# Projections in steps of three matmuls, a solve one slot later, and PSUM tiles read by one engine each, in a hybrid RWKV-7 and S5 block

## The chip, the cores and the metric

The kernel runs on one core of one Trainium2 chip. The metric is device time in microseconds (us) of one execution, and less is better. Before the change the median of three runs is 2781.7 us (2778.65 to 2786.51).

## The reference, cut to what matters

One layer on 2048 frames of width 1024: a norm, one wide input projection, an RWKV-7 branch (16 heads of 64), an S5 branch, gates, output projections and a residual. Nearly all matmul work is projections; the change lies around the chunked form of the RWKV-7 recurrence.

```python
h = rms_norm(x, norm_g[l]); z = h @ w_in[l]
zs, gate_a, u, gate_b, m_a, m_b = jnp.split(z, SPLIT_POINTS, axis=-1)
...
def frame_step(S, inp):                      # wkv7: 2048 frames in order
    r_t, w_t, k_t, v_t, a_t, b_t = inp
    sa = jnp.einsum('bhij,bhj->bhi', S, a_t)
    S = S * w_t[:, :, None, :] + sa[..., None] * b_t[:, :, None, :] + v_t[..., None] * k_t[:, :, None, :]
    return S, jnp.einsum('bhij,bhj->bhi', S, r_t)
...
merged = sigmoid(m_a) * (y_a @ p_a[l]) + sigmoid(m_b) * (y_b @ p_b[l])
x = x + merged @ w_out[l]
```

## The kernel before

The RWKV branch is cut into 32 units: a pair of heads p (8 pairs, 128 channels) by a block of 512 frames (4 blocks, two at a time). A unit is eight chunks of 64 frames. The driver loop at the end of the kernel goes over units, and for each over 24 **slots**. In a slot it emits, in this order: one step of `scan` of this unit, one step of `prep2` of the next unit, at some slots a step of `sums`, one step of `prep1` of the unit after that (from slot 13, P1) and of `post2` of the unit before, and then projection matmuls out of the generator `gm`, which `stream` makes of a list of jobs. Every engine runs its instructions in the order in which they are emitted, so what stands in a slot on TensorE (PE), VectorE (DVE) and ScalarE (ACT) is set by this loop; waits between engines come from the tiles that they share.

**scan** is the recurrence, three slots to a chunk. Slot 0, 3, 6, ...: matmul px from the state tile SU, which DVE copies to rh. Slot 1, 4, ...: matmul pu from rh; its two diagonal 64x64 blocks, scaled by dd, go into SU, the upper by DVE and the lower by ACT. Slot 2, 5, ...: matmul pn from SU; two DVE instructions make the next chunk's SU of it. So each slot's scan matmul needs what another engine made of the last slot's, and whatever PE has to do in a slot hides that.

**Projections** go out by `Job.run`: three 128x512 matmuls for each of 8 slices of the contraction (whi by hhi, whi by hlo, wlo by hhi), and a `yield` after every six. A slot takes one yield (six matmuls), the four slots in DOUBLE (1, 9, 15, 21) take two; 168 in a unit.

**prep2** prepares the next unit: transposes of BK (slot 1), two groups of 16 small matmuls into pairs of PSUM tiles A (slots 2 and 3), which are masked or scaled by dd into AT, then the DRAM round trip AT, ld, IX (slot 4), the product pv and the start of SU (slot 5), and from slot 6 a **solve**: 62 DVE instructions on TM, RF and IX that `Woven` puts between other DVE instructions, six a slot (SOLVE). At slot 16 the result RF goes to DRAM (rd) and back as R; after GAP slots, at slot 20, DVE transposes R into T, one half there and the other in slot 21; in slots 22 and 23 come small matmuls pz and pr. The tiles of the pool `psm` (tag m: A, sums, pv, pz and others) turn over three PSUM buffers.

**sums** makes column sums (slot 3), copies them to rows, the upper 32 rows by DVE and the lower by ACT (slot 4), sends them through DRAM and ends with a product on POOL.

## Time and profile before

| | us |
|---|---|
| median of three runs | 2781.7 |
| the profiled execution | 2781.73 |
| its span, first to last instruction | 2780.0 |
| PE busy | 2577.7 |
| DVE busy | 1923.0 |
| ACT busy | 1409.1 |
| POOL busy | 632.4 |

The units take from about 148 us to about 2170 us of the span; what is before is the first norm and projections, what is after is the S5 branch and the output projections. A timeline row gives start, duration, engine, line, operation, tiles and shapes, and in brackets the idle time before it and who ended it. An `xN` in it merges N instructions of one kind. A row of a view by line gives busy time, the mean of one instruction and the idle time just before.

### The profile page before, as it was taken

How to read it: one execution, taken by the hardware profiler on the slowest of the kernel's cores; microseconds unless marked ns; L12 is line 12 of the kernel's file. 1: busy time of each engine (PE TensorE's matmuls, PEld its weight loads, DVE VectorE, ACT ScalarE, POOL GpSimd, SP SyncE). 2: the span in 40 equal slices, each digit the busy share in tenths (PEclk: the TensorE clock that was granted, in tenths of full speed). 3: DMA queues.
4: the chain of work that ended last, by engine and by line, in shares of the span. 5: the costliest groups of instructions: out<-in, count | busy, mean ns of one | idle time of the engine just before them, and what ended most of it. 6: DMA issues, size and time to landing. Idle time of an engine off the chain costs nothing. (4 is left out here: it accounts for less than half of the span.)

```text
span 2780.0 us, 47342 instructions
## 1 busy us (share of the span) xinstructions
PE 2577.7 (93%) x16140; PEld 2044.4 (74%) x16140; DVE 1923.0 (69%) x5620; ACT 1409.1 (51%) x3547; POOL 632.4 (23%) x989
## 2 busy tenths in 40 slices
PE   6999999999999988999999999999989989999998
PEld 5777777777777766777777777777767777777777
DVE  5656677777667777766777766677768788755544
ACT  6455555555555665655555555555544443423321
POOL 3221222122222333222222122221332200111110
PEclk9999999999999999999999999999999999999999
DMA  3322333232232433333323232332466656755533
GB/s 110 78 77 66 92 77 99 70 85 78 75 92 69 136 116 100 89 82 83 86 75 92 72 90 74 88 91 71 110 180 183 212 139 168 227 185 173 168 108 98
DMA packets 256343, 303.42 MB, mean 109 GB/s; under 512 B 159745, under 2 KB 172134, under 8 KB 255078
## 3 DMA queue, kind: packets, MB, share of 16 engines
q1 hardware_dynamic: 210502, 150.94, 20.1%
q0 software_dynamic: 45600, 149.46, 18.1%
q8 instruction: 128, 2.10, 0.3%
q14 instruction: 113, 0.93, 0.1%
HBM read 219.91 MB, written 71.70 MB: 105 GB/s over the span
## 5 line engine op out<-in xcount | busy, mean ns | idle before, releaser
L950 ACT ACTIVATE SU<-pu,dd 64x64 f32<-64x64 f32 x256 | 79.0, 308 | 401.7 <-DVE SU L75 302.6
L879 DVE TENSOR_TENSOR TM<-RF,IX 128x60 f32<-128x60 f32 (+24 forms) x992 | 236.7, 239 | 64.7 <-DMA IX<-ld 42.4
L883 DVE TENSOR_TENSOR RF<-RF,TM 128x60 f32<-128x60 f32 (+24 forms) x992 | 217.2, 219 | 28.6 <-DVE TM L879 0.4
L945 ACT ACTIVATE AR<-SU,dec 64x64 f32<-64x64 f32 x512 | 176.2, 344 | 75.3 <-DVE SU L961 67.7
L953 PEld LDWEIGHTS pn<-SU,BT 128*128 128x128 f32 x512 | 86.4, 191 | 130.2 <-ACT SU L950 119.4
L953 PE MATMUL pn<-SU,BT 128*128 128x128 f32 x512 | 112.6, 302 | 67.9 <-ACT SU L950 66.0
L75 DVE TENSOR_TENSOR AT<-A,amask 64x256 f32<-64x256 f32 (+1 forms) x256 | 102.3, 419 | 72.2 <-ACT AT L843 66.9
L961 DVE SCALAR_TENSOR_TENSOR SU<-pn,dec,AR 64x64 f32<-64x64 f32 x240 | 65.3, 272 | 116.7 <-PE pn L953 116.5
L940 PEld LDWEIGHTS px<-SU,AT 128*128 128x128 f32 x512 | 93.5, 193 | 70.5 <-issue 31.4
L75 DVE COPY rh<-px 128x128 f32<-128x128 f32 x256 | 74.0, 289 | 98.5 <-PE px L940 94.3
L948 PEld LDWEIGHTS pu<-rh,R 128*128 128x128 f32 x512 | 92.3, 189 | 57.6 <-DVE rh L75 37.2
L940 PE MATMUL px<-SU,AT 128*128 128x128 f32 x512 | 104.1, 285 | 31.1 <-DVE SU L75 29.9
L843 ACT ACTIVATE AT<-A,dd 64x64 f32<-64x64 f32 x512 | 116.5, 303 | 19.0 <-PE A L837 16.3
L948 PE MATMUL pu<-rh,R 128*128 128x128 f32 x512 | 103.4, 284 | 18.7 <-DVE rh L75 17.7
L491 PE MATMUL ppa<-yhi,whi_pa 128*128 128x512 f32 x256 | 115.8, 452 | 1.4 <-ACT whi_pa L224 1.4
L491 PE MATMUL pv<-hhi,whi_v 128*128 128x512 f32 x256 | 111.5, 436 | 2.0 <-ACT carry L444 2.0
L491 PE MATMUL pmb<-hhi,whi_mb 128*128 128x512 f32 x256 | 112.0, 438 | 0.0
L491 PE MATMUL pga<-hhi,whi_ga 128*128 128x512 f32 x256 | 111.2, 434 | 0.0
L491 PE MATMUL pk<-hhi,whi_k 128*128 128x512 f32 x256 | 110.3, 431 | 0.7 <-ACT carry L444 0.7
L491 PE MATMUL pr<-hhi,whi_r 128*128 128x512 f32 x256 | 110.5, 432 | 0.0
L491 PE MATMUL pma<-hhi,whi_ma 128*128 128x512 f32 x256 | 110.1, 430 | 0.0
L493 PE MATMUL ppa<-yhi,wlo_pa 128*128 128x512 f32 x256 | 104.4, 408 | 1.6 <-DVE wlo_pa L75 1.6
(376 smaller groups left out, 7947.2 us busy)
## 6 DMA issues: line engine op xcount, KB each, us to landing
IX<-ld SPq DMA_DIRECT2D x128, 128.0 KB
raw_pa<-in_p_a_dram POOLq DMA_DIRECT2D x64, 256.0 KB, 4.3
raw_mb<-in_w_in_dram POOLq DMA_DIRECT2D x50, 256.0 KB, 3.5
raw_r<-in_w_in_dram POOLq DMA_DIRECT2D x36, 256.0 KB, 3.8
raw_k<-in_w_in_dram POOLq DMA_DIRECT2D x36, 256.0 KB, 3.6
raw_v<-in_w_in_dram POOLq DMA_DIRECT2D x36, 256.0 KB, 3.4
raw_ga<-in_w_in_dram POOLq DMA_DIRECT2D x34, 256.0 KB, 3.4
ce<-cw SPq DMA_DIRECT2D x16, 514.0 KB
```

Source lines behind the costliest of these rows:

```text
L75: r = f(*a, **kw)
L491: pe.matmul(ps, hi[:, k, :], xhi[:, kk_, :], start=(kk_ == 0), stop=False)
L493: pe.matmul(ps, lo[:, k, :], xhi[:, kk_, :], start=False, stop=(kk_ == 7))
L843: act.activation(out=at[HS[h], c, 0, h, :], in_=pas[h][HS[h], i, 0:C], func=AF.Copy, scale=dd[HS[h], c:c + 1])
L879: raw_dve.tensor_tensor(out=tm[:, 0:na, 0:nt], in0=rf[:, 0:na, s:s + 1].to_broadcast([P, na, nt]), in1=ix[:, s:s + 1, s + 1:32].to_broadca ...
L883: raw_dve.tensor_tensor(out=rf[:, 0:na, s + 1:32], in0=rf[:, 0:na, s + 1:32], in1=tm[:, 0:na, 0:nt], op=ALU.add)
L940: pe.matmul(px[:, 0:P], at[:, c, 0].rearrange("p h t -> p (h t)"), cur, start=True, stop=True)
L945: act.activation(out=us[HS[h]], in_=cur[HS[h], HS[h]], func=AF.Copy, scale=dec[HS[h]])
L948: pe.matmul(pu[:, 0:P], r64[:, c].rearrange("p h t -> p (h t)"), rh, start=True, stop=True)
L950: act.activation(out=cur[64:128, 64:128], in_=pu[64:128, 64:128], func=AF.Copy, scale=dd[64:128, c:c + 1])
L953: pe.matmul(pn[:, 0:P], bt[:, c].rearrange("p h j -> p (h j)"), cur, start=True, stop=True)
L961: (raw_dve if h == 0 else dve).scalar_tensor_tensor(out=nxt, in0=pn[HS[h], HS[h]], scalar=dec[HS[h]], in1=us[HS[h]], op0=ALU.mult, op1=ALU ...
```

## The change

The driver takes projections in steps of three matmuls: `Job.run` yields "half" after the first and third slice of four, the table HALVES says how many steps of three each slot takes (three where it says nothing; still 56, that is 168 matmuls, in a unit), and a wrapper `Steps` skips the halves for callers that want six. The loading of IX is emitted one slot earlier, the solve begins one slot later (slot 7, so it ends in slot 17), and GAP falls from 4 to 3, so T stays at slot 20. Three pairs of PSUM readers become one: the blocks of pu go by ACT alone, the rows of sums by ACT alone, and the dd blocks of A by DVE, four chunks in one instruction where ACT used one for each. Two products go from POOL to DVE (rdec, rkb), and the third and fourth step of sums come a slot later.

```diff
-GAP = 4
+GAP = 3
-DOUBLE = (1, 9, 15, 21)
+HALVES = {1: 2, 2: 1, 3: 0, 4: 2, 13: 2, 17: 1, 22: 0, 23: 0}
...
@@ Job.run
                                     next(self.bg, None)
                                 yield
+                            elif k < 3:
+                                yield "half"
...
@@ stream
-                for y, _ in enumerate(j.run()):
+                y = -1
+                for part in j.run():
+                    if part:
+                        yield part
+                        continue
+                    y += 1
...
@@ sums
+            lo_, hi_ = 0 if b else 32, 64 if a else 32
+            act.copy(rows[lo_:hi_], ps[lo_:hi_])
             if b:
-                dve.tensor_copy(rows[0:32], ps[0:32])
                 sp.dma_start(out=sd[0:2, :], in_=rows[0:2, :])
             if a:
-                act.copy(rows[32:64], ps[32:64])
...
-                pool.tensor_tensor(out=rkv_, in0=rkb, in1=U[a]["v"], op=ALU.mult)
+                dve.tensor_tensor(out=rkv_, in0=rkb, in1=U[a]["v"], op=ALU.mult)
...
@@ prep2
-                    for i in range(4):
-                        c = 4 * c2 + i
-                        act.activation(out=at[HS[h], c, 0, h, :], in_=pas[h][HS[h], i, 0:C], func=AF.Copy, scale=dd[HS[h], c:c + 1])
+                    dve.tensor_tensor(out=at[HS[h], cs_, 0, h, :], in0=pas[h][HS[h], :, 0:C], in1=dd[HS[h], cs_].unsqueeze(2).to_broadcast([C, 4, C]), op=ALU.mult)
...
-                yield
-            ix = u1.tile([P, 32, 32], F32, tag="BK", name="IX" + n)
...
-            pool.tensor_tensor(out=ar[:, :, C:2 * C], in0=ar[:, :, C:2 * C], in1=u["rdec"].to_broadcast([P, NC, C]), op=ALU.mult)
-            yield
+                    ix = u1.tile([P, 32, 32], F32, tag="BK", name="IX" + n)
...
+                yield
+            dve.tensor_tensor(out=ar[:, :, C:2 * C], in0=ar[:, :, C:2 * C], in1=u["rdec"].to_broadcast([P, NC, C]), op=ALU.mult)
...
+            yield
+            yield
             dve.chain = solve()
...
@@ scan
-                dve.tensor_scalar(out=cur[0:64, 0:64], in0=pu[0:64, 0:64], scalar1=dd[0:64, c:c + 1], scalar2=None, op0=ALU.mult)
-                act.activation(out=cur[64:128, 64:128], in_=pu[64:128, 64:128], func=AF.Copy, scale=dd[64:128, c:c + 1])
+                for h in range(2):
+                    act.activation(out=cur[HS[h], HS[h]], in_=pu[HS[h], HS[h]], func=AF.Copy, scale=dd[HS[h], c:c + 1])
...
@@ the driver
-                    if slot in (3, 4, 6 if last else 7, 11):
+                    if slot in (3, 4, 6 if last else 8, 12):
...
-                        if next(gm, None):
+                        if gm.half() == 1:
                             break
                         credit -= 1
```

On PE, slot 7 of the thirteenth unit before the change: pu, six projection matmuls (L491 to L493, of the job that fills pmb), and slot 8's pn.

```order
L948 MATMUL pu_0_2_9934<-rh_0_2_9916,R_161 128x128
L491 MATMUL pmb_0_9950<-hhi_178,whi_mb_0_9871 128x512
L492 MATMUL pmb_0_9950<-hlo_179,whi_mb_0_9871 128x512
L493 MATMUL pmb_0_9950<-hhi_178,wlo_mb_0_9872 128x512
L491 MATMUL pmb_0_9950<-hhi_178,whi_mb_0_9871 128x512
L492 MATMUL pmb_0_9950<-hlo_179,whi_mb_0_9871 128x512
L493 MATMUL pmb_0_9950<-hhi_178,wlo_mb_0_9872 128x512
L953 MATMUL pn_0_2_9957<-SU_0_9194,BT_0_9053 128x128
```

The same slot of the same unit in the changed kernel, on PE:

```order
L969 MATMUL pu_0_2_9726<-rh_0_2_9710,R_161 128x128
L491 MATMUL pmb_0_9704<-hhi_178,whi_mb_1_9676 128x512
L492 MATMUL pmb_0_9704<-hlo_179,whi_mb_1_9676 128x512
L493 MATMUL pmb_0_9704<-hhi_178,wlo_mb_1_9677 128x512
L491 MATMUL pmb_0_9704<-hhi_178,whi_mb_1_9676 128x512
L492 MATMUL pmb_0_9704<-hlo_179,whi_mb_1_9676 128x512
L493 MATMUL pmb_0_9704<-hhi_178,wlo_mb_1_9677 128x512
L491 MATMUL pmb_0_9704<-hhi_178,whi_mb_1_9676 128x512
L492 MATMUL pmb_0_9704<-hlo_179,whi_mb_1_9676 128x512
L493 MATMUL pmb_0_9704<-hhi_178,wlo_mb_1_9677 128x512
L974 MATMUL pn_0_2_9753<-SU_0_8982,BT_0_8896 128x128
```

Between pu and pn stand nine projection matmuls now. The same holds for the other slots that HALVES does not name.

On DVE, slots 2 and 3 of that unit before the change: the two halves of the next SU, the four masked blocks of the first pair of tiles A, a weight's low part (wlo), and rh.

```order
L961 SCALAR_TENSOR_TENSOR SU_0_9194<-pn_0_0_9763,dec_0_8883,AR_0_8887 64x64
L75 SCALAR_TENSOR_TENSOR SU_0_9194<-pn_0_0_9763,dec_0_8883,AR_0_8887 64x64
L75 TENSOR_TENSOR AT_1_9720<-A_1_0_0_9767,amask 64x4x64
L75 TENSOR_TENSOR AT_1_9720<-A_1_0_0_9767,amask 128x4x64
L75 TENSOR_TENSOR AT_1_9720<-A_1_0_1_9768,amask 64x4x64
L75 TENSOR_TENSOR AT_1_9720<-A_1_0_1_9768,amask 128x4x64
L75 TENSOR_TENSOR wlo_mb_1_9757<-raw_mb_4_9547,whi_mb_1_9756 128x512
L75 COPY rh_0_1_9800<-px_0_1_9798 128x128
```

The same place in the changed kernel, on DVE:

```order
L982 SCALAR_TENSOR_TENSOR SU_0_8982<-pn_0_0_9575,dec_0_8735,AR_0_8739 64x64
L75 SCALAR_TENSOR_TENSOR SU_0_8982<-pn_0_0_9575,dec_0_8735,AR_0_8739 64x64
L75 TENSOR_TENSOR AT_1_9550<-A_1_0_0_9579,dd_1_9334 64x4x64
L75 TENSOR_TENSOR AT_1_9550<-A_1_0_0_9579,amask 64x4x64
L75 TENSOR_TENSOR AT_1_9550<-A_1_0_0_9579,amask 128x4x64
L75 TENSOR_TENSOR AT_1_9550<-A_1_0_1_9580,dd_1_9334 64x4x64
L75 TENSOR_TENSOR AT_1_9550<-A_1_0_1_9580,amask 64x4x64
L75 TENSOR_TENSOR AT_1_9550<-A_1_0_1_9580,amask 128x4x64
L75 COPY rh_0_1_9602<-px_0_1_9600 128x128
```

Each A tile now has three DVE readers in a row (the one by dd came from ACT) where it had two, and rh stands behind six of them.

On DVE, slots 20 and 21 of that unit before the change: the first half of T, a weight's low part, three instructions of `prep1`, and the rh that slot 22's pu needs.

```order
L75 STREAM_TRANSPOSE T_6_1_10263<-R_162 32x256
L75 TENSOR_TENSOR wlo_mb_1_10253<-raw_mb_4_10166,whi_mb_1_10252 128x512
L75 COPY dec_0_10267<-eG_0_10186 128x8
L75 SCALAR_TENSOR_TENSOR AR_0_10271<-zk_7_9525,pd_127,eG_0_10186 128x8x63
L75 TENSOR_SCALAR AR_0_10271<-zk_7_9525,pd_127 128x8
L75 COPY rh_0_7_10285<-px_0_7_10283 128x128
```

And in the changed kernel, from the weight's low part on:

```order
L75 TENSOR_TENSOR wlo_mb_1_10073<-raw_mb_4_9980,whi_mb_1_10072 128x512
L982 SCALAR_TENSOR_TENSOR SU_0_8982<-pn_0_6_10089,dec_0_8735,AR_0_8739 64x64
L75 SCALAR_TENSOR_TENSOR SU_0_8982<-pn_0_6_10089,dec_0_8735,AR_0_8739 64x64
L75 STREAM_TRANSPOSE T_6_1_10093<-R_162 32x256
L75 COPY dec_0_10096<-eG_0_9990 128x8
L75 SCALAR_TENSOR_TENSOR AR_0_10100<-zk_7_9358,pd_127,eG_0_9990 128x8x63
L75 TENSOR_SCALAR AR_0_10100<-zk_7_9358,pd_127 128x8
L75 COPY rh_0_7_10115<-px_0_7_10113 128x128
```

The weight's low part has moved ahead of T; the three instructions of `prep1` still stand between T and rh. The solve's last instruction, which starts the way of RF through DRAM to R and T, is emitted in slot 17 where it was in slot 16.

## Rows read from the trace of the kernel before

**Rows 1.** The page's first part: span, busy time and share of each engine.

```profile
span 2780.0 us, 47342 instructions
PE 2577.7 (93%) x16140; PEld 2044.4 (74%) x16140; DVE 1923.0 (69%) x5620; ACT 1409.1 (51%) x3547; POOL 632.4 (23%) x989
```

**Rows 2.** Waits of PE: waiting line, releaser; us in total, times, longest.

```profile
PE pn L953 <- ACT SU L950: 66.0, 70, 3.5
PE px L940 <- DVE SU L75: 29.9, 36, 3.1
PE pu L948 <- DVE rh L75: 17.7, 20, 2.9
PE A L837 <- ACT AT L843: 3.5, 5, 0.7
```

**Rows 3.** Timeline around a slot 7: pu, projections, both copies of its blocks, pn.

```profile
1188.11 0.38 PE L948 MATMUL pu<-rh,R 128*128 128x128 f32 x2
...
1188.57 0.40 PE L492 MATMUL pk<-hlo,whi_k 128*128 128x512 f32 x1
...
1188.80 0.39 PE L493 MATMUL pk<-hhi,wlo_k 128*128 128x512 f32 x1
...
1189.36 0.27 DVE L75 TENSOR_SCALAR SU<-pu,dd 64x64 f32<-64x64 f32 x1
...
1189.72 0.31 ACT L950 ACTIVATE SU<-pu,dd 64x64 f32<-64x64 f32 x1 [1.67 <-DVE TM L879]
...
1190.09 0.49 PE L953 MATMUL pn<-SU,BT 128*128 128x128 f32 x2 [0.20 <-ACT SU L950]
```

**Rows 4.** PE's timeline: first and last wait behind a slot that grows.

```profile
173.47 0.49 PE L953 MATMUL pn<-SU,BT 128*128 128x128 f32 x2 [2.15 <-ACT SU L950]
...
2157.42 0.49 PE L948 MATMUL pu<-rh,R 128*128 128x128 f32 x2 [0.20 <-DVE rh L75]
```

**Rows 5.** By line: count, then busy us, mean ns, then idle before and releasers.

```profile
L950 ACT ACTIVATE SU<-pu,dd 64x64 f32<-64x64 f32 x256 | 79.0, 308 | 401.7 <-DVE SU L75 302.6 <-DVE TM L879 72.2 <-DVE RF L883 12.2
```

**Rows 6.** Timeline of slots 2 and 3 of another unit: A groups and DVE's part.

```profile
586.81 1.16 PE L837 MATMUL A<-AR,BK 64*128 64x128 f32 x16
...
588.95 1.68 DVE L75 TENSOR_TENSOR AT<-A,amask 64x256 f32<-64x256 f32 x4 [1.43 <-ACT AT L843]
589.41 0.38 PE L940 MATMUL px<-SU,AT 128*128 128x128 f32 x2
589.72 1.37 PE L837 MATMUL A<-AR,BK 64*128 64x128 f32 x16
...
590.56 0.67 DVE L75 TENSOR_TENSOR wlo_r<-raw_r,whi_r 128x512 fp32r<-128x512 f32 x1
```

**Rows 7.** Timeline of the same unit, slots 16 to 22: solve, R, T, rh, pu.

```profile
620.22 0.38 PE L948 MATMUL pu<-rh,R 128*128 128x128 f32 x2
...
622.12 0.49 PE L953 MATMUL pn<-SU,BT 128*128 128x128 f32 x2
...
622.40 2.55 SPq L896 DMA_DIRECT2D rd<-RF  x4
...
624.74 0.38 PE L940 MATMUL px<-SU,AT 128*128 128x128 f32 x2
...
629.63 0.43 DVE L75 STREAM_TRANSPOSE T<-R 32x256 f32<-32x256 f32 x1
629.82 0.39 PE L940 MATMUL px<-SU,AT 128*128 128x128 f32 x2
...
631.63 1.86 DVE L75 TENSOR_SCALAR AR<-zk,pd 128x8 f32<-128x8 f32 x1
...
633.52 0.29 DVE L75 COPY rh<-px 128x128 f32<-128x128 f32 x1
...
633.87 0.49 PE L948 MATMUL pu<-rh,R 128*128 128x128 f32 x2 [0.87 <-DVE rh L75]
```

**Rows 8.** DVE's idle time before T, by what ended it: us, times.

```profile
  DMA R<-rd: 10.5, 8
```

More of the change, by code (lines that the diff above doesn't have):

```diff
@@ L544, in stream, with __init__, half, __next__ @@
             settle()
+        class Steps:
+            def __init__(self, g):
+                self.g = g
+            def half(self):
+                return next(self.g, None)
+            def __next__(self):
+                v = next(self.g)
+                while v == "half":
+                    v = next(self.g)
+                return v
         def with_bg(js, g, gap, end=True):
@@ L850, in prep2 @@
                             sp.dma_start(out=ld[h, b].rearrange("c s t -> s c t"), in_=at[s0:s0 + 32, :, 0, h, 32 * b:32 * b + 32])
+                    ix = u1.tile([P, 32, 32], F32, tag="BK", name="IX" + n)
+                    ldf = ld.rearrange("h b c s t -> (h b c) s t")
+                    for q in range(4):
+                        sp.dma_start(out=ix[32 * q:32 * q + 32], in_=ldf)
                 yield
-            ix = u1.tile([P, 32, 32], F32, tag="BK", name="IX" + n)
-            ldf = ld.rearrange("h b c s t -> (h b c) s t")
-            for q in range(4):
-                sp.dma_start(out=ix[32 * q:32 * q + 32], in_=ldf)
-            pool.tensor_tensor(out=ar[:, :, C:2 * C], in0=ar[:, :, C:2 * C], in1=u["rdec"].to_broadcast([P, NC, C]), op=ALU.mult)
-            yield
+            dve.tensor_tensor(out=ar[:, :, C:2 * C], in0=ar[:, :, C:2 * C], in1=u["rdec"].to_broadcast([P, NC, C]), op=ALU.mult)
             su = up.tile([P, NC, P], F32, tag="SU", name="SU" + n)
@@ L1520, in tile_rwkv7_s5_block @@
             lraw = lora_dma(0)
-            gm = stream(pro + pro2 + jobs)
+            gm = Steps(stream(pro + pro2 + jobs))
             while (0, 0, "v") not in Z:
@@ L1586, in tile_rwkv7_s5_block @@
                         ready = next(s5)
-                    credit += T32 if last else T31 if n == NU - 1 else T30 if n == NU - 2 else PRO if n < 0 else 1 + DOUBLE.count(slot) - SKIP.count(slot)
+                    credit += 2 * (T32 if last else T31 if n == NU - 1 else T30 if n == NU - 2 else PRO) if n < 0 or n > NU - 3 else HALVES.get(slot, 3)
                     while credit >= 1:
-                        if next(gm, None):
+                        if gm.half() == 1:
                             break
```

## The prediction

> **What bounds the kernel now.** I read the page's first part first: PE is busy in 2577.7 us of a span of 2780.0 [rows 1]. PE is the bound, and since the change keeps every matmul, it can only win from the 202 us in which PE is idle. The view of PE's waits says where they are [rows 2]: 66.0 us before pn, for ACT's part of SU; 29.9 us before px, for DVE's part of SU; 17.7 us before pu, for rh. That is 113.6 us in 126 waits, all of them inside the 32 units and all of one kind: the scan matmul of a slot comes to its turn before the other engine has handed over its operand. The reader should see in [rows 3] how it works: pu starts at 1188.11, six projections follow, and pn is held until 1190.09, because DVE copies its block of pu at 1189.36 and ACT its own only at 1189.72, when DVE is done. What PE has to do in a slot is the cover for this, and with six matmuls it is often too short. DVE with 1923.0 us and ACT with 1409.1 are below PE, so they matter through the moment at which they answer, not through their sums.
>
> **Steps of three.** Matmuls of a projection start 0.23 us apart (1188.57 to 1188.80 in [rows 3]), so three are 0.70 us. Thirteen of the 24 slots go from six to nine; 4 and 13 keep six, 2 and 17 fall to three, 3, 22 and 23 to none, 9, 15 and 21 from twelve to nine, and 1 from twelve to six. I went through PE's timeline of the 32 units and noted each wait over 0.15 us before a scan matmul with the slot ahead of it. 113 of them, 100.5 us together, stand behind a slot that grows; [rows 4] are the first and the last. The release comes from an engine that started on the scan matmul one slot before, so 0.70 us more cover shortens each by up to 0.70 us: what is left of the 113 is 42.0 us, 28.0 of it before pn. Term: 42.0 - 100.5 = **-58.5 us**. The bounds are 0 (if the releasing engine is itself pushed back by as much) and -100.5 (if fewer waits also bring the engines back in step). I take the plain subtraction, since DVE and ACT get no more work in these slots. The slots that shrink hold matmuls of their own (transposes, A, sums, pss, pz, outs), and behind them the trace has few waits, 14 with 13.7 us; the two places where this matters come below.
>
> **pu read by ACT alone.** Now the handover to pn is DVE's copy (0.27 us) and then ACT's (0.31) [rows 3]; then it is two of ACT's. What goes is DVE's queue. ACT stood idle 401.7 us before its 256 copies, and 302.6 + 72.2 + 12.2 = 387.0 of that was ended by DVE instructions [rows 5], 1.5 us for each; a second ACT copy gives 0.31 back, so SU is ready some 1.2 us sooner wherever DVE was late. Of the 28.0 us that the longer slots leave before pn I let 4 stand, for slots in which ACT is itself busy: **-24 us**. The ends are -28 and, if ACT was not waiting for DVE at all, 67 waits of pn by 0.31 us, +21.
>
> On this the Trainium skill has a rule. The two blocks of pu lie in different halves of the partitions, and the trace shows ACT starting only 0.09 us after DVE's end [rows 3]. The page "PSUM — Partial Sum Buffer", section "PSUM bank collisions raise a hardware error", says that engines get in each other's way only in the same bank and the same quadrant of 32 partitions. By that rule the two copies need not follow each other, and giving both to ACT would cost the +21 instead of bringing the -24; by the row they do follow each other, since the program makes one wait for the other. I go by the row and keep the rule's result as a rival.
>
> **A by DVE alone (slots 2 to 4).** The two groups of A take 16 matmuls each; each group fills two tiles, and three PSUM buffers go round. Each DVE instruction on A takes 1.68 / 4 = 0.42 us [rows 6]. With the dd block there are three for a tile, so the first tile is free 1.26 us after the first group's end and the second at 2.52. The nearest row for the new instruction is the masked block of the same shape in the same tile, so I use its 0.42. PE comes to the second group after three projections (0.70) and px (589.72 - 589.41 = 0.31), 1.01 us after the first group: it waits 0.25 us and a handover, some 0.35, and pv, which also moves up to slot 4 behind this, waits some 0.25 more for its buffer. 32 x 0.6 = 19 us, less the 3.5 that A waits now [rows 2]: **+15 us**. The ends are -3 (DVE keeps up) and, if a weight's low part of 0.67 us stands between, as at 590.56 [rows 6], 32 x 1.27 - 3.5 = +37.
>
> **A later solve and GAP 3 (slots 17 to 22).** In the unit of [rows 7] the solve's slot starts at 620.22, rd is issued 2.18 us later, and T starts 7.23 us after that. Slot 17 lasts 624.74 - 622.12 = 2.62 us, slots 18 to 20 together 629.82 - 624.74 = 5.08, slot 21 633.87 - 629.82 = 4.05, of which 0.87 is a wait. With the new counts these become 1.92, 7.18 and 2.48, so pu of slot 22 is due 11.58 us after slot 17's start. R's way starts in slot 17 now: T comes 2.18 + 7.23 = 9.4 us after that start. Behind T, DVE has three instructions of `prep1` and rh; the way from T's start to rh's end is 633.52 + 0.29 - 629.63 = 4.18 us, with a weight's low part in it (0.67) that moves ahead, and with the 1.86 us instruction at 631.63, which has only eight columns and which I count at 0.2 to 1.86. So rh ends 1.9 to 3.5 us after T, at 11.3 to 12.9, and pu waits 0 to 1.3 us, 0.7 in the middle: 32 x 0.7 = 22 us. Of the 13.7 us behind shrinking slots 9.6 are this wait today, in 9 units (the 0.87 of [rows 7] is one), so the term is **+12 us**. The ends are -10 (R is often there well before T takes it) and +54: in 8 units DVE waited for R, 10.5 us in all [rows 8], and with 1.3 us more in every unit the wait is 32 x 2.0 us.
>
> **Edits counted at nothing.** IX one slot earlier and the solve one later: only DVE and SP see it, and the DVE time it may free is in the terms above. SP's queue keeps its order: ld, IX, then the rows of sums. Rows of sums by one ACT copy: off the chain, hidden by slots 5 to 8, in which its DRAM round trip runs; without that cover it would hold the later steps of sums, which moved a slot. Two products from POOL to DVE: 64 instructions of a weight's size (0.67) are 43 us of DVE, against 256 scaling copies of 0.27 us (69 us) that leave it; no wait of PE names POOL. They stand in slots 4 and 12 behind rh, so the next DVE work that PE needs is two slots off; were it not, each would cost up to 0.67 us, 43 us in all. The phases outside the units keep their instructions.
>
> **Sum.** -58.5 - 24 + 15 + 12 = -55.5 us, against the profiled execution's own 2781.73 us, which is the median of the three (2781.7): **2726 us**.
>
> **Rivals.**
> *A holds up PE* (the +37): DVE is late in slots 2 to 4 in every unit. For it: three readers for a tile, and rh behind six of them. Against: DVE has no solve in these slots. 2726 + 22 = 2748 us.
> *More than subtraction*: with every scan wait short, DVE and ACT run in step with PE and most of the 42.0 us goes too, as does slot 22's. For it: IX, cmp and rkb no longer sit in DVE's queue ahead of the scan. Against: rows like the 2.15 of [rows 4] are longer than three matmuls. 2726 - 14 - 12 = 2700 us.
> *The halves did not wait for each other*, the page's rule: 2726 + 24 + 21 = 2771 us. Against it: 387.0 of 401.7 [rows 5].
> *Slower: R is late.* One place: T in slot 20 holds DVE, rh of slot 21 is behind it, and PE stands at pu in slot 22. It eats the other terms (-67.5) from 2.1 us a unit on, over today's 0.3. R has to come 1.7 us later than in [rows 7]; the eight waits of [rows 8] are 1.3 on the mean. At 2.8 us a unit the time is 2726 - 12 + 32 x 2.8 - 9.6 = 2794 us.
> *It does not do what it says*: the order of PE shows nine matmuls where there were six, so no chance is given.
>
> **How the numbers follow.** A measurement of this kernel can tell some 0.3% (8 us) from no change. Forecast 0.58 (2708 to 2742); A holds up PE 0.15; more than subtraction 0.11; halves 0.07, on the edge of no change; R late 0.09. Faster: 0.58 + 0.15 + 0.11 and a little of the halves, 0.85; same 0.07; slower 0.08. The range runs from 2695, below which only part of the third case lies, to 2768, above which the last two cases lie.
>
> **What would show it.** In the changed profile: the waits of pn for ACT fall from 66.0 us to under 15; px and pu together from 47.6 to 30 to 45, most of the latter in slot 22; ACT no longer idles before its pu copies for DVE; A and the later pv wait 10 to 25 us for DVE's AT; PE's busy time stays at 2578 within 10. It is wrong if pn's waits stay above 30 us, which would mean that ACT's own queue was the delay, or if the waits at pu exceed 70 us, which is R. If projections themselves start to wait for weights, a cause is at work that none of this names.

## The result, and the profile after

The changed kernel takes **2738.01 us** (median of four runs, 2736.97 to 2738.93), the kernel before 2784.11 us beside it; the ratio is 0.9836, with a 95% interval from 0.9817 to 0.9855. So it is 46 us faster, where 56 were forecast (2726 us), and inside the range. One run of an experiment below, the solve with seven operations a slot, took 3482.49 us at a granted clock of 0.655, where the others have some 0.98, and is left out of its median. The profiled execution took 2738.93 us with this span and busy time, to set against [rows 1]:

```profile
span 2737.2 us, 46715 instructions
...
PE 2572.0 (94%) x16140; PEld 2053.4 (75%) x16140; DVE 1899.9 (69%) x5524; ACT 1377.0 (50%) x3293; POOL 557.6 (20%) x925
```

PE's busy time moved by 5.7 us only, so most of the gain, 37 us, is idle time that went. PE's waits (waiting line, releaser; us in total, times, longest), against [rows 2]:

```profile
PE px L961 <- DVE SU L75: 30.9, 50, 2.3
PE pu L969 <- DVE rh L75: 23.4, 21, 2.5
...
PE pn L974 <- ACT SU L971: 10.7, 22, 1.5
PE A L859 <- ACT BT L852: 4.3, 9, 0.9
PE pv L491 <- ACT carry L444: 5.9, 5, 1.9
```

pn fell from 66.0 to 10.7 us; px stayed (29.9 to 30.9), pu rose (17.7 to 23.4), and no row of A names AT any more. ACT's copies of pu, against [rows 5], by line:

```profile
L971 ACT ACTIVATE SU<-pu,dd 64x64 f32<-64x64 f32 x512 | 158.3, 309 | 284.6 <-PE pu L969 277.1
```

There are twice as many, and the idle time before them is now ended by PE's pu, no longer by DVE. A slot 7 like that of [rows 3]: ACT starts 0.49 us after pu, both copies are done at 1162.42, and pn's turn comes 1.2 us later.

```profile
1161.29 0.38 PE L969 MATMUL pu<-rh,R 128*128 128x128 f32 x2
...
1161.78 0.64 ACT L971 ACTIVATE SU<-pu,dd 64x64 f32<-64x64 f32 x2
...
1163.61 0.38 PE L974 MATMUL pn<-SU,BT 128*128 128x128 f32 x2
```

To see where waits went and came, I summed from PE's timeline, for each kernel below, every idle time over 0.1 us by the slot in which it stands, over all 32 units. A wait of slot n is before slot n's scan matmul, so the projections of slot n - 1 are its cover; an "o" marks waits of other matmuls in that slot (A in 2 and 3, pv of `prep2` in 4, mostly accumulations of a projection in 9 and 21). The table doesn't hold the whole of a difference between two kernels: a projection matmul lasts 0.39 to 0.40 us in [rows 3] and the next starts 0.23 us after it, so some 0.16 us of each wait count as busy, and PE's busy time lies between 2554 and 2582 us in these traces. us:

| kernel | 2o | 3o | 4o | 5 | 8 | 9 | 9o | 11 | 12 | 15 | 18 | 19 | 21o | 22 |
|---|---|---|---|---|---|---|---|---|---|---|---|---|---|---|
| before | 3.5 | 6.7 | 0.0 | 1.4 | 36.3 | 5.8 | 0.0 | 17.8 | 19.0 | 6.2 | 0.0 | 0.2 | 0.0 | 10.0 |
| after | 5.7 | 0.0 | 0.0 | 1.3 | 2.8 | 8.2 | 6.4 | 0.1 | 3.7 | 2.0 | 11.0 | 12.9 | 8.3 | 8.8 |
| steps alone | 4.6 | 13.0 | 0.0 | 23.8 | 15.3 | 4.0 | 21.2 | 4.7 | 3.3 | 0.0 | 7.6 | 3.1 | 7.8 | 4.2 |
| all but the steps | 3.8 | 2.0 | 0.4 | 0.0 | 2.9 | 4.0 | 0.0 | 12.4 | 19.4 | 15.7 | 0.5 | 31.4 | 0.0 | 23.9 |
| pu by ACT alone | 3.6 | 7.7 | 0.0 | 3.0 | 4.2 | 44.7 | 0.0 | 2.5 | 28.5 | 4.7 | 0.4 | 1.5 | 0.0 | 13.7 |
| steps and A | 4.5 | 0.4 | 0.0 | 18.4 | 16.9 | 4.4 | 21.5 | 3.8 | 4.0 | 0.4 | 7.6 | 4.0 | 8.4 | 4.1 |
| after, A as before | 5.7 | 13.3 | 17.6 | 0.0 | 2.6 | 5.0 | 3.5 | 0.0 | 5.2 | 2.2 | 10.6 | 14.3 | 8.2 | 8.7 |
| after, solve early | 5.7 | 0.4 | 0.6 | 1.3 | 2.4 | 20.8 | 4.3 | 0.2 | 2.9 | 1.9 | 7.1 | 1.9 | 7.8 | 2.9 |
| after, pu by both | 4.3 | 0.4 | 0.6 | 0.6 | 5.6 | 6.0 | 4.7 | 6.4 | 2.7 | 0.5 | 11.9 | 12.3 | 8.2 | 9.2 |
| after, products on GpSimd | 5.6 | 0.4 | 0.6 | 1.3 | 3.9 | 8.4 | 4.1 | 0.6 | 5.7 | 0.9 | 11.1 | 15.2 | 8.4 | 9.1 |
| after, AR by DVE | 5.3 | 1.0 | 0.8 | 1.3 | 2.2 | 12.9 | 4.8 | 0.1 | 3.7 | 2.0 | 10.7 | 0.7 | 5.3 | 3.8 |

From before to after, slots 8, 11 and 12 lose 66.5 us of 73.1; slots 18, 19 and the "o" columns of 9 and 21 gain 38.4. The forecast had put the new waits into slots 2 to 4 and 22.

### The profile page after: what moved, and what is told of

It reads as the page before. It is cut to its first block, busy times and chain, and to the rows that moved or that the text cites. A ratio compares the mean times of both kernels' runs of the same rounds, so it can differ in the third digit from the quotient of the medians.

```text
span 2737.2 us, 46715 instructions
## 1 busy us (share of the span) xinstructions
PE 2572.0 (94%) x16140; PEld 2053.4 (75%) x16140; DVE 1899.9 (69%) x5524; ACT 1377.0 (50%) x3293; POOL 557.6 (20%) x925
## 5 line engine op out<-in xcount | busy, mean ns | idle before, releaser
L971 ACT ACTIVATE SU<-pu,dd 64x64 f32<-64x64 f32 x512 | 158.3, 309 | 284.6 <-PE pu L969 277.1
L898 DVE TENSOR_TENSOR TM<-RF,IX 128x60 f32<-128x60 f32 (+24 forms) x992 | 208.8, 210 | 65.7 <-DMA IX<-ld 44.9
L902 DVE TENSOR_TENSOR RF<-RF,TM 128x60 f32<-128x60 f32 (+24 forms) x992 | 224.6, 226 | 28.9
L961 PE MATMUL px<-SU,AT 128*128 128x128 f32 x512 | 108.0, 293 | 31.5 <-DVE SU L75 30.9
L969 PE MATMUL pu<-rh,R 128*128 128x128 f32 x512 | 106.7, 290 | 24.0 <-DVE rh L75 23.4
L974 PEld LDWEIGHTS pn<-SU,BT 128*128 128x128 f32 x512 | 92.2, 190 | 43.1 <-ACT SU L971 23.9
L491 PE MATMUL ppa<-yhi,whi_pa 128*128 128x512 f32 x256 | 115.6, 451 | 4.6 <-DVE sg L75 4.6
L974 PE MATMUL pn<-SU,BT 128*128 128x128 f32 x512 | 105.3, 288 | 11.4 <-ACT SU L971 10.7
L491 PE MATMUL pv<-hhi,whi_v 128*128 128x512 f32 x256 | 109.5, 428 | 6.7 <-ACT carry L444 5.9
L491 PE MATMUL pmb<-hhi,whi_mb 128*128 128x512 f32 x256 | 110.1, 430 | 0.0
L491 PE MATMUL pga<-hhi,whi_ga 128*128 128x512 f32 x256 | 108.9, 426 | 1.0 <-ACT carry L444 1.0
L491 PE MATMUL pk<-hhi,whi_k 128*128 128x512 f32 x256 | 109.6, 428 | 0.3
L491 PE MATMUL pr<-hhi,whi_r 128*128 128x512 f32 x256 | 109.3, 427 | 0.0
L491 PE MATMUL pma<-hhi,whi_ma 128*128 128x512 f32 x256 | 108.6, 424 | 0.0
L493 PE MATMUL ppa<-yhi,wlo_pa 128*128 128x512 f32 x256 | 103.8, 405 | 1.6 <-DVE wlo_pa L75 1.6
L492 PE MATMUL ppa<-ylo,whi_pa 128*128 128x512 f32 x256 | 103.9, 406 | 0.0
```

The costliest lines, as they stand in the source:

```text
L491: pe.matmul(ps, hi[:, k, :], xhi[:, kk_, :], start=(kk_ == 0), stop=False)
L492: pe.matmul(ps, hi[:, k, :], xlo[:, kk_, :], start=False, stop=False)
L493: pe.matmul(ps, lo[:, k, :], xhi[:, kk_, :], start=False, stop=(kk_ == 7))
L898: raw_dve.tensor_tensor(out=tm[:, 0:na, 0:nt], in0=rf[:, 0:na, s:s + 1].to_broadcast([P, na, nt]), in1=ix[:, s:s + 1, s + 1:32].to_broadca ...
L902: raw_dve.tensor_tensor(out=rf[:, 0:na, s + 1:32], in0=rf[:, 0:na, s + 1:32], in1=tm[:, 0:na, 0:nt], op=ALU.add)
L961: pe.matmul(px[:, 0:P], at[:, c, 0].rearrange("p h t -> p (h t)"), cur, start=True, stop=True)
```

## The experiments

The first seven take the change apart: some parts alone on the kernel before, and one part at a time taken back from the changed kernel.

**Steps of three alone.** The kernel before with `Steps` and HALVES.

```diff
-DOUBLE = (1, 9, 15, 21)
+HALVES = {1: 2, 2: 1, 3: 0, 4: 2, 13: 2, 17: 1, 22: 0, 23: 0}
...
+                            elif k < 3:
+                                yield "half"
```

> The kernel before with the steps of three and the table HALVES alone; the readers of PSUM tiles, the solve's place, GAP and POOL's products stay as before. Theory S (steps are the cover that was missing; the prediction's first term): waits before scan matmuls fall from 113.6 us to 50 to 65, of which 20 to 35 before pn, and the time to 2725 to 2740 us. Theory P (the pair of engines on pu is what held pn, longer slots only move the wait): pn's waits stay above 45 us, the time is 2755 to 2775 us.

Measured: 2790.53 us, ratio 1.0014 (1.0 to 1.0027). The part that was to bring the most brings nothing by itself. PE's waits:

```profile
PE pn L975 <- ACT SU L972: 48.7, 55, 2.5
PE pv L491 <- ACT carry L444: 22.1, 12, 2.6
...
PE A L859 <- ACT AT L865: 13.0, 30, 1.6
```

By slots (the table) the longer slots do what was said: 8, 11 and 12 go from 73.1 to 23.3 us, 50 us less. But slot 5 gets 22.4 more, the projection in slot 9 21.2, A in slot 3 6.3, slots 18, 19 and 21 18.3: 68 us come back. (The slots not named here lose some 15 us, so PE's waits in the units are 3 us more in all, 172.1 in place of 168.8.) Slots 2 and 3 have three matmuls and none where they had six each, so DVE and ACT have that much less time for A, and are late to pu's copies for slot 5 as well. Both theories had a gain, and both missed.

**All but the steps.** The changed kernel with steps of six and DOUBLE again (the first diff turned round).

> The changed kernel without the steps: six matmuls a slot and twelve in slots 1, 9, 15 and 21 as before, all other parts of the change kept. Theory S: pn's waits only fall to 40 to 50 us, px and pu keep theirs or gain from the later solve, the time is 2760 to 2785 us. Theory P: pn's waits fall under 20 us and the time is 2735 to 2750 us, near the changed kernel's 2738.

Measured: 2781.55 us, ratio 0.9988 (0.9971 to 1.0005): the rest alone brings nothing either. PE's waits:

```profile
PE pu L962 <- DVE rh L75: 61.9, 56, 3.9
PE px L954 <- DVE SU L75: 39.1, 42, 4.9
PE pn L967 <- ACT SU L964: 21.4, 35, 3.1
```

pn is down by two thirds, and pu up from 17.7 to 61.9, 55 us of waits are now in slots 19 and 22. Neither half of the change is worth anything without the other: taken from the changed kernel, the steps are worth 43.5 us.

**pu by ACT alone, on the kernel before.**

```diff
-                dve.tensor_scalar(out=cur[0:64, 0:64], in0=pu[0:64, 0:64], ...)
-                act.activation(out=cur[64:128, 64:128], in_=pu[64:128, 64:128], ...)
+                for h in range(2):
+                    act.activation(out=cur[HS[h], HS[h]], in_=pu[HS[h], HS[h]], ...)
```

> The kernel before with one edit: both blocks of pu by ACT. If ACT's copy waits for DVE's, pn's waits fall from 66.0 to 25 to 45 us and the time to 2745 to 2765 us. If the halves did not wait for each other, pn's waits grow by 0.31 us each to some 85 us and the time is 2790 to 2810 us.

Measured: 2778.98 us, ratio 0.9985 (0.9966 to 1.0003): no difference that can be told, and neither of the two ranges. PE's waits show the wait handed on, not removed:

```profile
PE px L940 <- DVE SU L75: 78.8, 64, 3.9
...
PE pn L953 <- ACT SU L950: 14.9, 30, 2.2
```

pn fell by 51.1 us, px rose by 48.9. In the table slot 8 falls from 36.3 to 4.2 us and slot 9 rises from 5.8 to 44.7. What stands behind both is DVE's queue, held by the solve's first operations, which wait for IX to arrive by DMA. In the kernel before, this is the unit of the first wait in [rows 4]:

```profile
171.89 0.19 DVE L879 TENSOR_TENSOR TM<-RF,IX 128x31 f32<-128x31 f32 x1 [2.29 <-DMA IX<-ld]
...
172.75 0.27 DVE L75 TENSOR_SCALAR SU<-pu,dd 64x64 f32<-64x64 f32 x1
...
173.11 0.31 ACT L950 ACTIVATE SU<-pu,dd 64x64 f32<-64x64 f32 x1 [3.62 <-DVE TM L879]
```

DVE stands for 2.29 us, its copy of pu comes late, ACT's follows it, and pn waits 2.15 us. By the timeline 24 of the 26 waits in slot 8, 33.5 of the 36.3 us, come within 4.5 us behind such a stall. With ACT reading pu, pn is free of DVE's queue, but px is not, since DVE makes its SU: here 20 of the 28 waits in slot 9, 36.4 of the 44.7 us, come within 4.5 us behind a stall for IX.

**pu by both engines, in the changed kernel** (the last diff turned round).

> The changed kernel, but pu's blocks are copied by DVE and ACT as before. The prediction's second term says that this gives 24 us back: 2755 to 2765 us, with 25 to 35 us of waits at pn where the changed kernel has 10.7. The rival: with nine matmuls in a slot the pair is fast enough, pn's waits stay under 16 us and the time is 2733 to 2744 us. The third, that the halves never waited for each other: 2715 to 2732 us, since one ACT copy of 0.31 us falls away.

Measured: 2750.34 us, ratio 0.987 (0.9856 to 0.9884). Here ACT alone is worth 12.3 us, and PE's row of pn is

```profile
PE pn L974 <- ACT SU L971: 22.4, 33, 3.5
```

where it was 10.7. That this is nearly the same number is chance: px gives 4.8 us back, all of PE's waits in the units rise by 1.6 us only (from 128.5 to 130.1), and PE's busy time by 8.9. By slots the cost stands where pn waits: slots 8 and 11 rise by 9.1 us.

**The solve at its old place, in the changed kernel.** It begins in slot 6, with GAP 4.

```diff
-GAP = 3
+GAP = 4
...
-            yield
             yield
             dve.chain = solve()
```

> The changed kernel with the solve starting in slot 6 and GAP 4, as before; IX keeps its new, earlier place, T stays at slot 20. In the changed kernel's trace 24 us of waits stand before px of slot 18 and pu of slot 19, where the kernel before had none to speak of. Theory L (the solve's end now meets prep1's DVE work in slots 17 and 18): those waits go, 2710 to 2724 us. Rival K (slot 17 got only three matmuls and is too short): they stay, 2732 to 2744 us. A third: the solve then waits for IX and pays in slots 6 to 9 what it wins later, 2735 to 2745 us with over 25 us of waits in those slots.

Measured: **2714.65 us**, ratio 0.9741 (0.9716 to 0.9766), better than both kernels. The later solve costs 23.4 us. PE's waits:

```profile
PE px L960 <- DVE SU L75: 38.1, 34, 4.7
...
PE pu L968 <- DVE rh L75: 7.6, 6, 2.9
```

pu fell from 23.4 to 7.6 us. Of the waits, slots 18, 19 and 22 lost 20.8 us and slot 9 gained 12.6, where DVE, early with the solve, stands before IX: DVE's row for IX rose from 44.9 to 68.0 us, and 17.2 of slot 9's 20.8 us come within 4.5 us behind such a stall. In the changed kernel these are 4.5 of 8.2 us.

**A by both engines, in the changed kernel.**

```diff
-                    dve.tensor_tensor(out=at[HS[h], cs_, 0, h, :], in0=pas[h][HS[h], :, 0:C], in1=dd..., op=ALU.mult)
+                    for i in range(4):
+                        c = 4 * c2 + i
+                        act.activation(out=at[HS[h], c, 0, h, :], in_=pas[h][HS[h], i, 0:C], func=AF.Copy, scale=dd...)
```

> The changed kernel, but the dd blocks of A by ACT, four instructions for a tile, as before. The prediction's third term holds that DVE alone costs 15 us here: 2718 to 2728 us. What the changed kernel's trace suggests (no wait of PE for DVE's AT): 2735 to 2745 us; above 2745 if ACT's load, 5 us more a unit, holds pn's operand.

Measured: 2769.23 us, ratio 0.9939 (0.9917 to 0.996). A by DVE is a gain of 31.2 us in the changed kernel. The time is in the highest range expected, but not for pn, whose row is 9.8 us; PE's waits name AT, in nearly every unit:

```profile
PE pv L883 <- ACT AT L865: 17.6, 29, 1.1
...
PE A L859 <- ACT AT L865: 12.9, 30, 1.6
```

**Both products on GpSimd, in the changed kernel.** rkv and AR<-AR,rdec are issued by `pool` again, not by `dve`.

> The changed kernel with both products back on POOL. The prediction counted them at nothing: 2732 to 2744 us. If DVE instructions stand still while a POOL product runs, as one did for 1.86 us in the trace of before, DVE loses some 1 us twice a unit at slots 4 to 12: 2745 to 2765 us.

Measured: 2749.97 us, ratio 0.987 (0.9848 to 0.9892): by the medians moving them was worth 12.0 us, but the interval overlaps with that of the changed kernel (0.9817 to 0.9855), so that there is a gain is likely and its size open. What the products cost on GpSimd is seen on DVE, in the lines of the solve (busy us, mean ns):

```profile
L898 DVE TENSOR_TENSOR TM<-RF,IX 128x60 f32<-128x60 f32 (+24 forms) x992 | 243.5, 245 | 60.4 <-DMA IX<-ld 39.4
L902 DVE TENSOR_TENSOR RF<-RF,TM 128x60 f32<-128x60 f32 (+24 forms) x992 | 230.0, 232 | 29.9
```

Together 473.5 us; the changed kernel has 433.4 for the same instructions. 38 of the 1984 took over 0.5 us, against 12 in the changed kernel, where about 0.2 is usual. How much of this reaches PE isn't shown: its waits in the units rise by 1.7 us only (from 128.5 to 130.2), and its busy time by 9.5, at a granted clock of 0.978 in this trace and 0.982 in that of the changed kernel.

**Another table of steps.** The changed kernel with slot 17 at two steps and slot 1 at one, to see if slot 17, at one step, is too short for px of slot 18.

```diff
-HALVES = {1: 2, 2: 1, 3: 0, 4: 2, 13: 2, 17: 1, 22: 0, 23: 0}
+HALVES = {1: 1, 2: 1, 3: 0, 4: 2, 13: 2, 17: 2, 22: 0, 23: 0}
```

> The changed kernel with three matmuls moved from slot 1 to slot 17 (slot 17 six, slot 1 three). Rival K (slot 17 too short): the 11 us before px of slot 18 go, and some of the 13 us before pu of slot 19: 2718 to 2728 us. Theory L (DVE's work, not slot 17's length): the waits at slot 18 go but those at slot 19 stay or grow, 2728 to 2738 us. Slot 1 with only three matmuls might hold pn of slot 2 for ACT's copies: then up to 10 us more.

Measured: 2748.34 us, ratio 0.9867 (0.9844 to 0.9891), 10 us worse than the changed kernel. By slots: 18 falls from 11.0 to 1.4 us and 19 from 12.9 to 9.5, so slot 17 was indeed short for px; but A behind the shorter slot 1 goes from 5.7 to 15.5, and slot 22 from 8.8 to 13.4. The run changes two slots at once, so it does not price slot 17 alone; it shows that three matmuls taken from slot 1 are missed there.

**Steps and A by DVE.** Why do the steps need the rest? The first guess was ACT's sixteen multiplications of A. The kernel before with the steps and with A by DVE (the two diffs above).

> The kernel before with the steps of three (and HALVES) and with A copied by VectorE alone; pu on two engines, the solve at its old place, the products on GpSimd. Theory G (steps and A belong together): with the steps alone the growing slots 8, 11 and 12 gave back 50 us (73 to 23), but 57 us of waits stood elsewhere, pn of slot 5 behind ScalarE 23.8, the projection's pv in slot 9 behind ScalarE's carry 20.2, the second half of A in slot 3 behind ScalarE's AT 13.0, and in the changed kernel these three are 0, 5.6 and 0. If what they wait behind is ScalarE's sixteen small multiplications of A, they go here too: 2730 to 2760 us, A's row for AT under 2 us, pn of slot 5 under 5 us. Rival H (what freed them was ScalarE's other work, or the product off GpSimd): A's own 13 us goes, the other two stay: 2772 to 2785 us.

Measured: 2767.2 us, ratio 0.9934 (0.9915 to 0.9953): 23 us better than the steps alone, and between the two expectations. A's own waits in slot 3 go (13.0 to 0.4), as both said; slots 5 and 9 keep theirs (18.4 and 21.5), as H said. So A is a part of what the steps need, and not all. The timeline of a slot 4 shows what holds slot 5:

```profile
645.47 0.49 PE L968 MATMUL pu<-rh,R 128*128 128x128 f32 x2
...
646.93 0.73 DVE L75 SCALAR_TENSOR_TENSOR zv<-pv,prm,zv 128x511 f32<-128x511 f32 x1
...
647.71 0.27 DVE L75 TENSOR_SCALAR SU<-pu,dd 64x64 f32<-64x64 f32 x1
647.82 0.16 ACT L444 COPY carry<-pv 128x1 f32<-128x1 f32 x1 [3.61 <-DVE zv L75]
...
648.08 0.31 ACT L970 ACTIVATE SU<-pu,dd 64x64 f32<-64x64 f32 x1
648.44 0.49 PE L973 MATMUL pn<-SU,BT 128*128 128x128 f32 x2 [1.06 <-ACT SU L970]
648.76 0.50 PE L882 MATMUL pv<-cen,zv 128*128 128x128 f32 x3
```

SU is ready 2.9 us after pu, behind DVE's copies of A and ACT's carry. In the changed kernel it is no earlier, as this timeline of the same place shows:

```profile
636.97 0.49 PE L969 MATMUL pu<-rh,R 128*128 128x128 f32 x2
...
637.41 1.13 PE L881 MATMUL pv<-cen,zv 128*128 128x128 f32 x8
...
639.32 0.16 ACT L444 COPY carry<-pv 128x1 f32<-128x1 f32 x1 [3.64 <-DVE zv L75]
639.50 0.64 ACT L971 ACTIVATE SU<-pu,dd 64x64 f32<-64x64 f32 x2
...
640.20 0.49 PE L974 MATMUL pn<-SU,BT 128*128 128x128 f32 x2 [0.26 <-ACT SU L971]
```

It takes 3.2 us, but the eight pv matmuls of `prep2`, 1.13 us, now stand between pu and pn: the slot that was freed by loading IX earlier moved them from slot 5 to slot 4, and they cover the wait. The edit that I had counted at nothing is worth these 18 us or so, read from the timeline; it was not run alone. That slot 5 keeps 0.0 to 1.3 us in the four kernels of the table that take the later solve, pu, A or the products back from the changed kernel says that none of these alone freed it; pv's slot, IX and the edits in `sums` are what is left. Slot 9's wait has another cause: in the timeline of one unit two of the solve's operations, which already stand in DVE's queue there, take 1.24 and 1.18 us, while GpSimd works through two DMA issues (1432.82 to 1434.39) and a product (1434.40 to 1435.70), and the second part of zk, its carry and so the projection's next accumulation come late. With the products back on GpSimd in the changed kernel this wait does not return (4.1 us), so what took it away there is not settled.

**A by DVE alone, on the kernel before.**

> The kernel before with A copied by VectorE alone, nothing else. Theory G: in the kernel before, VectorE waits 66.9 us for ScalarE's multiplications of A, but TensorE itself waits only about 7 us at A and has two projection matmuls behind it in the same slots, so the copy by VectorE has nothing to give without the steps: 2770 to 2790 us. Rival J (A by VectorE is a gain of its own, since taking it back from the changed kernel cost 28 us): 2745 to 2765 us.

Measured: 2780.15 us, ratio 0.9981 (0.9966 to 0.9997): some 5 us, and at most 9. DVE's waits of the kernel before say how much DVE stood behind ACT at A:

```profile
DVE AT L75 <- ACT AT L843: 66.9, 62, 6.2
```

Those 66.9 us are real, but with six projections in slots 2 and 3 PE did not need AT sooner. With three and none, as the steps leave them, it does: 23 us with the steps, 31 us with the whole change.

**Seven operations of the solve a slot, in the changed kernel.** The solve begins as late as there and ends two slots earlier, in slot 15.

```diff
-SOLVE = 6
-GAP = 3
+SOLVE = 7
+GAP = 5
```

> The changed kernel with the solve at its new, later place, but seven of its operations a slot instead of six (GAP 5, so that what follows R stays where it is): the solve is done two slots earlier, in slots 8 to 16 instead of 8 to 18. Theory L (what the later solve costs is its end, beside px and pu of slots 18 and 19, 24 us there): the waits of slots 18 and 19 fall from 24 us to under 10, and with the solve's start after IX has landed the kernel gets to 2705 to 2725 us, as with the early solve (2715). Rival M (VectorE is too full for seven: the waits go to the slots 9 to 15): 2730 to 2755 us.

Measured: 2722.59 us (median of three), ratio 0.9773 (0.975 to 0.9796). Slots 18 and 19 fall from 23.9 to 10.2 us, slot 22 from 8.8 to 2.3; slots 9, 12 and 14 give 11 us back (from 15.2 to 26.6). So most of the cost is at the solve's end, as theory L had it, if not quite under its 10 us for slots 18 and 19.

**One product of the setup by DVE, in the changed kernel.** The solve's end in the changed kernel, in a unit where pu of slot 19 waits:

```profile
313.02 0.56 POOL L628 DMA_DIRECT2D gb_d<-exgb  x1 [1.33 <-DVE SU L982]
...
313.35 1.73 DVE L902 TENSOR_TENSOR RF<-RF,TM 128x16 f32<-128x16 f32 x1
...
313.57 0.20 POOL L755 COPY rdec<-G 128x8 f32<-128x8 f32 x1
313.74 1.30 POOL L760 TENSOR_TENSOR AR<-zr,eG 128x512 f32<-128x512 f32 x1
315.11 0.18 DVE L898 TENSOR_TENSOR TM<-RF,IX 128x8 f32<-128x8 f32 x1
...
317.06 0.29 DVE L75 COPY rh<-px 128x128 f32<-128x128 f32 x1
...
317.41 0.49 PE L969 MATMUL pu<-rh,R 128*128 128x128 f32 x2 [1.38 <-DVE rh L75]
```

A solve operation on 16 columns takes 1.73 us, until 0.04 us after GpSimd's product is done; kh, dd, the reciprocal and rh queue behind it, and pu waits 1.38. Ten of the eleven waits of over 0.5 us in slot 19 have such a row before them. The solve one slot earlier, or seven a slot, is done before that product. The run takes the product off GpSimd and leaves the solve where it is.

```diff
-            pool.tensor_tensor(out=ar[:, :, C:2 * C], in0=c3(r), in1=c3(eg), op=ALU.mult)
+            dve.tensor_tensor(out=ar[:, :, C:2 * C], in0=c3(r), in1=c3(eg), op=ALU.mult)
```

> The changed kernel with one product of the unit's setup, AR<-zr,eG (128x512, 1.28 us on GpSimd, 32 of them), computed by VectorE; the solve stays at its later place. In the changed kernel ten of the eleven waits of pu in slot 19, and the long ones of px in slot 18, stand right behind a solve operation that took 1.7 us in place of 0.2 while that product ran on GpSimd; 12 solve operations of the span were that long, 17.3 us over their usual time, and with the solve early or seven a slot there were none. Theory N (what the later solve costs in slots 18 and 19 is VectorE held up by GpSimd's product, not VectorE's own work there): solve operations of over 0.5 us fall from 12 to about none, the waits of slots 18 and 19 from 24 to under 12 us, and the kernel gets to 2718 to 2732 us. Rival O (VectorE's own work in slot 17, the last solve operations with kh, dd and the reciprocal, is what is late, and 0.7 us of product more makes it later): the waits of slots 18 and 19 stay at 20 to 40 us: 2736 to 2760 us.

Measured: 2720.01 us, ratio 0.9766 (0.9738 to 0.9794). DVE's solve lines and, below, PE's waits:

```profile
L902 DVE TENSOR_TENSOR RF<-RF,TM 128x60 f32<-128x60 f32 (+24 forms) x992 | 208.3, 210 | 28.9
L898 DVE TENSOR_TENSOR TM<-RF,IX 128x60 f32<-128x60 f32 (+24 forms) x992 | 208.2, 210 | 68.3 <-DMA IX<-ld 45.7 <-issue 1.8
```

```profile
PE pu L969 <- DVE rh L75: 6.2, 7, 2.6
```

No solve operation is over 0.5 us any more, slot 19 falls from 12.9 to 0.7 us and slot 22 from 8.8 to 3.8, although DVE has 0.69 us more to do in every unit; slots 9 and 23 gain some 10 us. So theory N holds for pu, and not for px. Slot 18 stays at 10.7: px's wait there is not the product, and by the run with slot 17 at two steps it is that slot's length. In the unit above px of slot 18 started at 313.46, before the long operation had ended.

## Why the prediction was right, and where not

The time came out 12 us above the forecast because errors of both signs met, so that it lies inside the range is in good part luck; as a sum of independent terms the forecast was wrong.

**Steps of three, -58.5.** At its own slots the subtraction holds: 50 us less in slots 8, 11 and 12 with the steps alone. The step that failed is the sentence on the slots that shrink, that behind them "the trace has few waits, 14 with 13.7 us" (one of these, in slot 5, stands behind slot 4, which keeps its six). The trace of before shows waits under the cover as it was. With three matmuls in place of six in slot 2 and none in slot 3, A and slot 5 began to wait; with slot 9 and the slots after 17, 68 us came back. Taken from the finished kernel, the steps are worth 43.5 us.

**pu by ACT alone, -24.** Right in kind, half the size: 12.3 us in the changed kernel, nothing on the kernel before, where px took the wait over. The rival by which the halves did not wait for each other is out: with two readers, pn's row rises from 10.7 to 22.4 us, and in none of the 256 pairs of the trace, nor of that of before, does ACT's copy start until DVE's has ended, 0.09 us after it in the median. What the term missed is what made DVE late, the stall for IX: with ACT alone on the kernel before, px waits behind it in place of pn. The rule of the Trainium skill ("PSUM — Partial Sum Buffer", section "PSUM bank collisions raise a hardware error"), that different quadrants can be read at once, is no price of this program's wait, in which one copy follows the other all the same; whether for the tile pu or for SU, no run shows.

**A by DVE alone, +15.** The sign is wrong, it is -31. Two steps failed. First the base: I set the new copies against the 3.5 us that A waited in the kernel before, and not against what ACT's copies would have cost in the new, shorter slots, which are 13.3 us in slot 3 and 17.6 in slot 4. Second the 0.25 us by which PE was to be early. This timeline of the changed kernel shows DVE starting 0.13 us before the first group's modelled end, so that three instructions (0.42 and 0.86) free the first tile at 693.04, with the second group begun at 692.92 and no wait shown; by the order of the tiles its first matmul goes to the third buffer, and the second, at 693.14, is the first to need the freed one:

```profile
690.56 1.32 PE L859 MATMUL A<-AR,BK 64*128 64x128 f32 x16
...
691.75 0.42 DVE L75 TENSOR_TENSOR AT<-A,dd 64x256 f32<-64x256 f32 x1 [0.48 <-PE A L859]
692.18 0.86 DVE L75 TENSOR_TENSOR AT<-A,amask 64x256 f32<-64x256 f32 x2
692.61 0.39 PE L961 MATMUL px<-SU,AT 128*128 128x128 f32 x2
692.92 1.39 PE L859 MATMUL A<-AR,BK 64*128 64x128 f32 x16
```

**A later solve and GAP 3, +12.** The sign is right and the size is half: 23.4 us. The place is mostly wrong. Slot 22 went from 10.0 to 8.8 us, where it was to go up; DVE's wait for R, [rows 8], is little changed:

```profile
  DMA R<-rd: 13.5, 9
```

Against the run with the early solve, slot 22 has 5.9 us more, so a part of the cost does stand there, but not for R: with the product by DVE, DVE's wait for R is 16.4 us and slot 22 has 3.8. The rest of the cost, 14.9 us, is in slots 18 and 19. I had followed R and not the solve's own last operations, which moved beside `prep1` and its product on GpSimd. The 1.86 us instruction of [rows 7], on eight columns, was the clue: GpSimd's AR<-zr,eG ran from 632.19 to 633.46 in that trace, and the instruction ended at 633.49. I counted it at "0.2 to 1.86" and did not ask what held it.

**Edits counted at nothing.** Three were not nothing, as far as can be told. Two products off GpSimd are worth 12.0 us by the medians, with the doubt said above; I weighed the DVE time that they take and not the DVE time that they hold up on GpSimd. And the slot that IX freed gave pv to slot 4 as a cover; I had put pv's move down as a place of waiting. And IX earlier with the solve later bears on the stall behind the largest wait: slot 9 has 44.7 us with pu by ACT alone and 4.0 with all but the steps, which also has pu by ACT. These two differ in other edits too, and slots 19 and 22 rise from 15.2 to 55.3 us between them, so no run prices it.

**What would show it.** pn under 15 us: 10.7. ACT no longer idle for DVE before its copies: so it is. PE's busy time within 10 of 2578: 2572.0. px and pu together at 30 to 45 us, most in slot 22: 54.3, mostly in slots 9, 18 and 19, a miss. A and pv waiting 10 to 25 us for DVE's AT: none, a miss.

**The sum.** Each part taken back from the changed kernel: steps 43.5, A 31.2, pu 12.3, products 12.0, the later solve -23.4. They add up to 75.6 us where the change brings 46.1, and steps and rest alone bring nothing each. (By the ratios, each against the kernel before as measured beside it, they are some 42, 29, 9.5, 9.5 and -26, 64 us together.) The parts share waits: what one removes at one slot, another has to cover at the next. What is not settled: the price of pv's earlier slot alone, the price of IX earlier alone, whether the products' hold-up reaches PE, the exact share of slot 17's length, and why other matmuls than the scan's still wait some 15 us in slots 9 and 21, 7 of them projections for carry.

## What to carry to other kernels

When a table of cover is moved, look at the slots that get less as closely as at those that get more: a wait that the trace does not show may just be covered, and each part is to be priced in the arrangement that the others make, not in the old one. A wait that goes from one matmul to the next (pn to px here) is the sign that what holds both stands further back, here a queue behind a DMA, so that a quicker link alone brings nothing. An instruction of a few columns that takes many times its usual time is worth a question at once: here it named the engine to unload.

## What the runs showed of the hardware

VectorE's instructions on SBUF were held up while GpSimd worked through a product. In the changed kernel 12 of the solve's 1984 operations took 1.3 to 1.7 us in place of 0.2, and with two more products on GpSimd 38 took over 0.5; with the solve out of the way of the product, or the product by VectorE, there were none, and the solve's lines went from 433.4 to 416.5 us. The Trainium skill says as much ("SBUF — State Buffer", section "SBUF: two separate sides") of a VectorE operation with two inputs in SBUF, as the solve's are, beside a GpSimd operation that reads SBUF: the two engines share a port pair, taken whole by one instruction at a time while the other stands. It also says that whichever starts first gets it. The trace doesn't show that order: by it the VectorE operation at 313.35 began 0.39 us before the product at 313.74 and still ended only after it; a DMA issue and a small copy on GpSimd lay directly ahead of the product, so it may have lost its turn to GpSimd's queue three times over, which no run here takes apart.
